# Gate operands and the stored product on GpSimd's queue, and the last gate tile in two column halves: a hybrid encoder block on one core

## The chip, the cores and the metric

The kernel runs on one core of a Trainium2 chip. The core has a matrix engine (TensorE, PE in the profile, with PEld for its weight loads), a vector engine (VectorE, DVE), a scalar engine (ScalarE, ACT), GpSimd (POOL) and SyncE (SP), each with its own queue of instructions that it works off in order. SP computes nothing here; it issues DMAs. POOL can issue DMAs too. Whoever issues them, 16 DMA engines move the data. The metric is the device time of one execution in microseconds; lower is better.

## What is computed

The reference is one encoder block over 1024 tokens of width 1024: windowed attention and a recurrent mixer side by side, an output projection, a feed-forward part, and at the end a gated input embedding. The change touches the two last parts, which are:

```python
        x = x + merged @ w_out[i]
        hf = rms_norm(x, norm_ffn[i])
        x = x + jnp.square(jax.nn.relu(hf @ w_ff1[i])) @ w_ff2[i]
        hp = rms_norm(x, norm_ple[i])
        x = x + (p[i] @ w_ple[i]) * jax.nn.sigmoid(hp @ w_ple_gate[i])
```

Here `w_ff2` is 4096 x 1024, `w_ple_gate` is 1024 x 1024, `p` is 1024 x 256 and `w_ple` is 256 x 1024.

## The kernel before

**Products.** All data are float32. Each matrix operand is split into a high part (ACT casts it, L205) and a low part (DVE subtracts, L206), and a product is three matmuls: high by high, high by low, low by high. The three large products at the end are done as block products with seven multiplications instead of eight (quarter blocks B11 to B22 and sums of them, named T1 to T4 and S1 to S4).

**Second feed-forward product** (from about 1210 us to 1530 us). Seven products (`PRODS`, numbered `ip` 0 to 6) run one after the other, each over 16 steps p. A step fetches a left tile of hidden values from DRAM (`sst`, three slots, L1834 in `fetch`), splits it into `sh` and `sl`, makes the right tile from a fetched weight block (`tst`, three slots) or from sums that are kept on the chip, splits it into `th` and `tl`, and runs 12 matmuls (L2024) on it. The split tiles have five slots each (`NR2`). After a product, DVE adds its four banks to the residual `X` (L1881).

**Gate operands.** The seven right operands of the gate product depend on weights alone. They are made while products 1 to 4 run: the generator `gate_operands` is advanced by one piece after some of the steps. A piece loads a raw block of 128 x 512 (`graw`, three slots, L1896), or forms a sum on DVE (`gsum`, two slots), and `keep` splits it with the same `th` and `tl` slots and stores the two parts in DRAM (`gop_d`, L1900). In all there are 16 loads and 56 stores of 256 KB. During product 6 and later they are loaded again (L1962, on SP's queue).

**Stored product.** During product 6, `ple_product` computes `p @ w_ple` for eight groups of tokens, and ACT scales it by 0.5 (L2006). The 16 results go to DRAM (`pw_d`, L2007).

**Gate product and end** (from about 1555 us). `product_of` runs 12 matmuls into one bank, for each of four groups of 128 tokens and each product. `finish` does the rest for a tile of 128 tokens by 512 columns, 16 times: it loads the stored product (`pwl`, three slots, L2112), applies tanh on ACT (L2113), multiplies on DVE (L2114), adds to `X` on DVE (L2115), and stores the output (L2116). `add_bank` (L2105) adds the last bank to the kept partial sum before that. The sigmoid is written as (tanh(x/2) + 1)/2, and the factor one half is in the stored product.

**Order.** The program is traced in the order of the code; a planner then lays out each engine's queue from dependencies, slots and its own costs, so instructions of different steps are mixed, and it also picks the slot of each tile. Matmuls marked by `keep_in_program_order` (`mmo`) stay in the order of the code. A queue is worked off in order: a DMA that waits for its data or for a free slot holds all DMAs behind it on that queue. Before the change, SP's queue holds the fetches of the feed-forward product, the gate loads and stores, the stored product in both directions, and the output. POOL's queue holds at this stage only the small `rstd` steps of the last norm (L189). Earlier in the kernel POOL issues some DMAs as well (L226, L413, L415, L777, L929).

Of the kernel before, what the change touches and what calls it, by code (L numbers as in the profile page):

```python
# [9 lines left out]
F32 = mybir.dt.float32  # L10
F32R = mybir.dt.float32r
AF = mybir.ActivationFunctionType
ALU = mybir.AluOpType
# [4 lines left out]
P = 128  # L18
# [131 lines left out]
def block_kernel(ctx: ExitStack, tc: tile.TileContext, I: dict, out: bass.AP):  # L150
    nc = tc.nc

    def pool(stack, name, bufs=1, **kw):
        return stack.enter_context(tc.tile_pool(name=name, bufs=bufs, reuse_waits="tile", **kw))
# [20 lines left out]
    gop_d = {r: DR.tile([2, P, 4, 512], F32, name="gop_" + r) for r in ("T1", "T4", "B11", "T2", "T3", "B22", "B21")}  # L175
    pw_d = DR.tile([NT, 2, P, 512], F32, name="pw_d")
# [69 lines left out]
    def mm3(ps, pairs):  # L246

        n = len(pairs)
        for i, (ah, al, bh, bl) in enumerate(pairs):
            nc.tensor.matmul(ps, ah, bh, start=(i == 0), stop=False)  # L250
            nc.tensor.matmul(ps, ah, bl, start=False, stop=False)  # L251
            nc.tensor.matmul(ps, al, bh, start=False, stop=(i == n - 1))  # L252
# [95 lines left out]
    with ExitStack() as s0:  # L348
# [51 lines left out]
        parts = []  # L400
# [50 lines left out]
        for t in range(NT):  # L451
# [34 lines left out]
            r = QW.tile([P, NQK], F32, name="r2", bufs=2)  # L486
# [433 lines left out]
    with ExitStack() as s2:  # L920
# [16 lines left out]
        for n in range(NT):  # L937
# [5 lines left out]
            for kv in range(2):  # L943
# [6 lines left out]
                for h in range(4):  # L950
                    sc = PA.tile([P, nk * P], F32, name="sc", tag="sc", bufs=2)
                    for j in range(2):
                        nc.tensor.matmul(sc, qT[:, 4 * kv + h, :], kT[:, kv, j, k0 * P:k1 * P], start=(j == 0), stop=(j == 1))
                    nc.vector.tensor_tensor_reduce(
                        out=sm[:, h, 0:nk * P], in0=sc, in1=band[:, b0:b0 + nk, :].rearrange("p b t -> p (b t)"), scale=1.0,
                        scalar=-3.0e38, op0=ALU.add, op1=ALU.max, accum_out=mx[:, h:h + 1])
# [629 lines left out]
    with ExitStack() as s7:  # L1586
# [15 lines left out]
        for j, i in enumerate((4, 5, 6, 7, 0, 1, 2, 3)):  # L1602
            t = torder[i]
# [10 lines left out]
        raw = [NR.tile([P, 4, 512], F32, name=f"raw{k}", bufs=1) for k in range(2)]  # L1614
# [50 lines left out]
        for i in range(NT):  # L1665
# [6 lines left out]
            t = torder[i]  # L1672
# [23 lines left out]
    def tmp(name, bufs=1):  # L1696
        return FP.tile([P, 512], F32, name=name, bufs=bufs)
# [58 lines left out]
    for p in range(NPR):  # L1756
# [13 lines left out]
        else:  # L1770
            s_ = tmp("u2")
# [55 lines left out]
    def parts_of(pl, names, src_, bufs):  # L1827
        hi, lo = (pl.tile([P, 512], F32R, name=x_, bufs=bufs) for x_ in names)
        split(hi, lo, src_)
        return hi, lo  # L1830
# [20 lines left out]
    def acc(bs, name="ff2ps"):  # L1851
        return PH.tile([P, 512], F32, name=name, tag=f"acc{bs}", bufs=4)

    def sum_of(op, a_, b_, out_=None):
        o_ = F2.tile([P, 512], F32, name="tmp", bufs=2) if out_ is None else out_
        nc.vector.tensor_tensor(out=o_, in0=a_, in1=b_, op=op)
        return o_
# [28 lines left out]
    def gate_block(k, b):  # L1886
        r = (k + 4 * (int(b[1]) - 1)) * P
        n = 512 * (int(b[2]) - 1)
        return I["w_ple_gate"][r:r + P, n:n + 512]

    def gate_operands():

        def load(k, b):
            if k < 4:
                raw[b] = QP.tile([P, 512], F32, name="graw", tag="graw", bufs=3)
                nc.sync.dma_start(raw[b], gate_block(k, b))  # L1896

        def keep(k, r, src_):
            for x_, t_ in enumerate(parts_of(F2, ("th", "tl"), src_, NR2)):
                nc.sync.dma_start(gop_d[r][x_][:, k, :], t_.bitcast(F32))  # L1900

        def gsum():
            return QP.tile([P, 512], F32, name="gsum", tag="gsum", bufs=2)

        raw = {}
        for b in ("B11", "B12", "B22"):
            load(0, b)
        yield
        for k in range(4):
            t = sum_of(ALU.subtract, raw["B12"], raw["B11"], gsum())  # L1910
            keep(k, "T1", t)
            yield
            keep(k, "B11", raw["B11"])
            load(k, "B21")
            yield
            keep(k, "T3", sum_of(ALU.subtract, raw["B22"], raw["B12"], gsum()))
            load(k + 1, "B11")
            yield
            sum_of(ALU.subtract, raw["B22"], t, t)
            keep(k, "T2", t)  # L1920
            yield
            keep(k, "B22", raw["B22"])
            load(k + 1, "B12")
            yield
            sum_of(ALU.subtract, raw["B21"], t, t)
            keep(k, "T4", t)
            yield
            keep(k, "B21", raw["B21"])
            load(k + 1, "B22")
            yield  # L1930

    def tok(e, i):
        t = torder[4 * e + i]
        return X[e][:, i, :], slice(t * P, (t + 1) * P), t
# [64 lines left out]
    def ple_product(k, pp):  # L1999

        for n in range(2):
            pw = acc(1, "pwps")
            nsl = slice(512 * n, 512 * n + 512)
            mm3(pw, [(pp[0][:, j, :], pp[1][:, j, :], wp[0][:, j, nsl], wp[1][:, j, nsl]) for j in range(2)])
            t_ = F2.tile([P, 512], F32, name="pwt", tag="tmp", bufs=2)
            nc.scalar.activation(out=t_, in_=pw, func=AF.Copy, scale=0.5)  # L2006
            nc.sync.dma_start(pw_d[k, n], t_)  # L2007

    gops = gate_operands()
    GL, GR = {}, {}  # L2010
# [1 line left out]
    for ip, (lr_, rr_, bs, fresh) in enumerate(PRODS):  # L2012
        if fresh:
            banks[bs] = [acc(bs) for _ in range(4)]
        for p in range(NPR):
# [25 lines left out]
            if ip == 1 and p % 2 == 0:  # L2041
                e, i = divmod(p // 2, 4)
                t = torder[4 * e + i]
# [8 lines left out]
            if ip == 5 and p % 4 == 1:  # L2052
                k, nsl = p // 8, slice(512 * (p // 4 % 2), 512 * (p // 4 % 2) + 512)
                split(wp[0][:, k, nsl], wp[1][:, k, nsl], fetch(F2, wpv[:, k, nsl], "tst", 3))
            if ip == 6:
                next(gl[p // 8], None)
                if p % 2 == 0 and p < 8:
                    ple_norm(1, p // 2)
                if p % 2 == 1 and 2 < p < 11:
                    second_tokens((p - 3) // 2)  # L2060
                if p >= 7:
                    pps.append(ple_p(p - 7)) if p < 15 else None
                    if p > 7:
                        ple_product(p - 8, pps[p - 8])
        for i in range(4):
            b_ = banks[bs][i]
# [26 lines left out]
    LP = pool(sF, "gate2")  # L2093
    GL["A11"], GR["B11"] = left(LP, 2), gate_loaded(LP, 2, "B11")
    g12 = LP.tile([P, 4, 512], F32, name="g12", bufs=1)
    cs_ = {n: [LP.tile([P, 512], F32, name=n, tag=f"{n}{i}", bufs=1) for i in range(4)] for n in ("gc5", "gc4", "gc1", "gu2")}

    def product_of(bank, l, r, i, fresh=True):
        (lh, ll), (rh, rl) = GL[l], GR[r]
        for k in range(4):  # L2100
            for j, (x_, y_) in enumerate(((lh, rh), (lh, rl), (ll, rh))):
                mmo(bank, x_[:, k, tsl(i)], y_[:, k, :], start=fresh and k + j == 0, stop=k == 3 and j == 2, skip_group_check=True)

    def add_bank(n, i, bank):
        nc.vector.tensor_tensor(out=cs_[n][i], in0=cs_[n][i], in1=bank, op=ALU.add)  # L2105

    def finish(e, n, i, c):

        xv, rows, t = tok(e, i)
        nsl = slice(512 * n, 512 * n + 512)  # L2110
        pw = LP.tile([P, 512], F32, name="pwl", bufs=3)
        nc.sync.dma_start(pw, pw_d[t, n])  # L2112
        nc.scalar.activation(out=c, in_=c, func=AF.Tanh, scale=0.5)  # L2113
        nc.vector.scalar_tensor_tensor(out=c, in0=c, scalar=1.0, in1=pw, op0=ALU.add, op1=ALU.mult)  # L2114
        nc.vector.tensor_tensor(out=xv[:, nsl], in0=xv[:, nsl], in1=c, op=ALU.add)  # L2115
        nc.sync.dma_start(out[rows, nsl], xv[:, nsl])  # L2116

    R4 = range(4)
    ple_norm(0, 0)
# [1 line left out]
    kept = [acc(1, "gps5") for _ in R4]  # L2121
# [8 lines left out]
    for i in R4:  # L2130
        b_ = acc(0, "gps4")
# [6 lines left out]
    chain = [acc(0, "gps1") for _ in R4]  # L2138
# [15 lines left out]
    for i in R4:  # L2154
        product_of(chain[i], "S3", "T3", i, False)
        for e, n, c in ((1, 1, "gc5"), (1, 0, "gc4")):
            add_bank(c, i, chain[i])
            finish(e, n, i, cs_[c][i])
    for i in R4:
        product_of(kept[i], "S4", "B22", i, False)  # L2160
        add_bank("gu2", i, kept[i])
        finish(0, 1, i, cs_["gu2"][i])
    for i in R4:
        b_ = acc(0, "gps2")
        product_of(b_, "A12", "B21", i)
        add_bank("gc1", i, b_)
        finish(0, 0, i, cs_["gc1"][i])
    sF.close()
    sRP.close()
    sX.close()  # L2170
# [25 lines left out]
```

## Time and profile before

| | us |
|---|---|
| median of three runs | 1649.55 |
| lowest and highest run | 1646.11, 1649.56 |
| the profiled execution | 1649.13 |
| its span, first to last instruction | 1647.4 |
| PE busy in the span | 1595.4 |
| mean granted clock of TensorE | 0.991 of full speed |

The profile is of one execution. Its span is shorter than its time by what lies around it. PE's share of the span, 97%, is an average: most stretches have no gap at all, and a few have all of them. Windows of 20 us show which. A row of the table of windows gives the busy time and the number of instructions of each engine, and then the granted clock, the share of the DMA engines and the bytes moved in GB/s. A row of the timeline gives start, duration, engine, line, operation and tiles; brackets hold the idle time of that engine before it and what ended it. A row of waits gives who waited for whom: total, times and the longest.

### The profile page before, as it was taken

The numbers are of one execution on the slowest core, as the hardware profiler recorded it, in microseconds if no ns is written. First come the engines' busy times: TensorE is split into PE (matmuls) and PEld (weight loads), VectorE is DVE, ScalarE is ACT, GpSimd is POOL, SyncE is SP. The second block draws the span as 40 slices with busy tenths as digits, with TensorE's granted clock in tenths as the row PEclk, the third lists the DMA queues.
The fourth block names the chain that finished last, engine by engine and source line by source line (L and its number), as shares of the span: only waits on it lengthen the run. The fifth ranks groups of instructions, "written<-read, shape, count | busy, mean of one in ns | idle before, by whom it ended". The sixth has DMA issues, their size and how long they took to land.

```text
span 1647.4 us, 31465 instructions
## 1 busy us (share of the span) xinstructions
PE 1595.4 (97%) x12232; PEld 1289.4 (78%) x12232; DVE 1176.3 (71%) x2161; ACT 874.5 (53%) x1615; POOL 84.6 (5%) x110
## 2 busy tenths in 40 slices
PE   7999999999999999899999999999999999999998
PEld 7987777767768777667888788888888778788886
DVE  6758998378849769688737876676758868777257
ACT  5558888388554563655314544444444444546352
POOL 1430000300000000000001000000000000000000
PEclk9999999999989999999999999999999999999999
DMA  6363555964575744567822354444479887768356
GB/s 228 84 159 109 167 166 180 274 165 141 157 198 172 217 147 130 165 194 247 271 79 92 119 169 156 159 145 145 151 261 315 278 275 239 238 218 286 125 198 236
DMA packets 218678, 307.02 MB, mean 186 GB/s; under 512 B 49824, under 2 KB 106016, under 8 KB 217248
## 3 DMA queue, kind: packets, MB, share of 16 engines
q1 hardware_dynamic: 207312, 287.70, 53.8%
q0 software_dynamic: 11072, 16.78, 3.8%
q8 instruction: 96, 1.57, 0.4%
q10 hardware_dynamic: 144, 0.52, 0.1%
q14 instruction: 54, 0.44, 0.1%
HBM read 205.33 MB, written 99.61 MB: 185 GB/s over the span
## 4 chain that ended last, share of the span: by engine, by line
PE 66%; DVE 16%; DMA 8%; ACT 6%; issue 3%; POOL 1%; SPq 0%; DVEq 0%; ACTq 0%; POOLq 0%
PE ff1ps L1694 16%; PE ff2ps L2024 12%; PE gps L232 4%; PE uaps L232 2%; DMA wst<-in_w_col_dram 2%; DVE Z L1346 2%; DVE tmp L1343 2%; PE mm L250 2%; DMA tst<-in_w_ff_dram 2%; PE mm L251 2%; PE mm L252 2%; PE gmm L232 2%; PE mmo L251 1%; PE mmo L252 1%; PE mmo L250 1%
## 5 line engine op out<-in xcount | busy, mean ns | idle before, releaser
L2024 PE MATMUL ff2ps<-th,sh 128*128 128x512 f32 x448 | 177.2, 396 | 5.7 <-ACT th L205 5.7
L2024 PE MATMUL ff2ps<-tl,sh 128*128 128x512 f32 x448 | 178.0, 397 | 4.1 <-DVE tl L206 4.0
L2024 PE MATMUL ff2ps<-th,sl 128*128 128x512 f32 x448 | 176.6, 394 | 0.0
L2024 PEld LDWEIGHTS ff2ps<-th,sh 128*128 128x128 f32 x448 | 85.4, 191 | 25.7 <-ACT th L205 7.7
L2024 PEld LDWEIGHTS ff2ps<-tl,sh 128*128 128x128 f32 x448 | 85.4, 191 | 24.8 <-DVE tl L206 6.9
L205 ACT CAST whi<-wst 128x512 fp32r<-128x512 f32 x100 | 60.0, 618 | 83.6 <-DMA wst<-in_w_col_dram 34.1
L205 ACT CAST sh<-sst 128x512 fp32r<-128x512 f32 x109 | 67.2, 619 | 62.8 <-DMA sst<-hid_A 22.2
L2024 PEld LDWEIGHTS ff2ps<-th,sl 128*128 128x128 f32 x448 | 85.7, 191 | 17.7
L206 DVE TENSOR_TENSOR sl<-sst,sh 128x512 fp32r<-128x512 f32 x109 | 74.7, 687 | 24.0 <-ACT sh L205 23.6
L1694 PE MATMUL ff1ps<-mh,w1h 128*128 128x512 f32 x224 | 87.5, 391 | 0.2 <-ACT w1h L205 0.2
L1694 PE MATMUL ff1ps<-ml,w1h 128*128 128x512 f32 x224 | 87.4, 390 | 0.0
L1694 PE MATMUL ff1ps<-mh,w1l 128*128 128x512 f32 x224 | 87.2, 389 | 0.0
L205 ACT CAST w1h<-w1st 128x512 fp32r<-128x512 f32 x48 | 28.4, 620 | 99.8 <-DMA w1st<-in_w_ff_dram 62.0
L206 DVE TENSOR_TENSOR wlo<-wst,whi 128x512 fp32r<-128x512 f32 x88 | 58.9, 685 | 16.9 <-ACT whi L205 14.8
L206 DVE TENSOR_TENSOR w1l<-w1st,w1h 128x512 fp32r<-128x512 f32 x48 | 31.9, 687 | 51.3 <-ACT w1h L205 51.3
L189 POOL TENSOR_TENSOR rstd<-ms,neghalf 128x1 f32<-128x1 f32 x24 | 15.4, 643 | 1000.5 <-issue 589.3
L1208 DVE TENSOR_TENSOR gm<-gps,gmask 128x384 f32<-128x384 f32 x64 | 32.8, 551 | 31.0 <-PE gps L232 30.9
L232 PE MATMUL gmm<-hh,wlo 128*128 128x512 f32 x128 | 53.4, 417 | 0.0
L238 PE MATMUL gmm<-hh,whi 128*128 128x512 f32 x128 | 51.5, 402 | 1.7 <-ACT whi L205 1.7
L232 PE MATMUL gmm<-hl,whi 128*128 128x512 f32 x128 | 53.2, 415 | 0.0
L206 DVE TENSOR_TENSOR w1l<-ssum,w1h 128x512 fp32r<-128x512 f32 x64 | 42.9, 687 | 14.3 <-ACT w1h L205 14.3
L232 PE MATMUL gmm<-hh,whi 128*128 128x512 f32 x128 | 53.0, 414 | 0.0
(463 smaller groups left out, 4593.8 us busy)
## 6 DMA issues: line engine op xcount, KB each, us to landing
tst<-in_w_ff_dram SPq DMA_DIRECT2D x80, 256.0 KB, 4.5
wst<-in_w_col_dram SPq DMA_DIRECT2D x76, 256.0 KB, 3.8
w1st<-in_w_ff_dram SPq DMA_DIRECT2D x32, 512.0 KB, 4.9
hid_S<-h SPq DMA_DIRECT2D x64, 256.0 KB, 2.1
sst<-hid_S SPq DMA_DIRECT2D x64, 256.0 KB, 4.2
hid_A<-h SPq DMA_DIRECT2D x48, 256.0 KB, 2.0
sst<-hid_A SPq DMA_DIRECT2D x45, 256.0 KB, 4.2
ra_d<-ra SPq DMA_DIRECT2D x8, 1024.0 KB, 5.9
```

The lines of the kernel that those rows point to most:

```text
L205: a = nc.scalar.copy(hi, src)
L206: b = (lo_eng or nc.vector).tensor_tensor(out=lo, in0=src, in1=hi.bitcast(F32), op=ALU.subtract)
L232: tc.keep_in_program_order(nc.tensor.matmul(*a, **kw))
L238: mm(ps, ah, bh, start=(i == 0), stop=False)
L250: nc.tensor.matmul(ps, ah, bh, start=(i == 0), stop=False)
L251: nc.tensor.matmul(ps, ah, bl, start=False, stop=False)
L252: nc.tensor.matmul(ps, al, bh, start=False, stop=(i == n - 1))
L1208: a = (nc.vector.tensor_tensor(out=gm[hf][:, s % NB, e].rearrange("p (a b) t -> p a b t", b=2), in0=pss[e][:, 0:6].rearrange("p (a b) t -> ...
L1343: turn(nc.vector.tensor_tensor(out=tv, in0=Lp[:, t + 1:32, t:t + 1].broadcast_to([P, n, m]), in1=Z[:, t:t + 1, 0:m].broadcast_to([P, n, m] ...
L1346: turn(nc.vector.tensor_tensor(out=Z[:, t + 1:32, 0:m], in0=Z[:, t + 1:32, 0:m], in1=tv, op=ALU.add))
L1694: (mmo if p < 2 else nc.tensor.matmul)(ps, x_[:, k, :], y_[:, k, :], start=start and k + i == 0, stop=k == 3 and i == 2, skip_group_check= ...
L2024: nc.tensor.matmul(banks[bs][i], x_[:, isl], y_, start=fresh and p + j == 0, stop=p == NPR - 1 and j == 2, skip_group_check=True)
```

## The change

The loads of raw gate blocks, the stores of gate operands, and the stores and loads of the stored product are issued by GpSimd (POOL) instead of SP. `add_bank` is folded into `finish`, which issues the load of the stored product ahead of the add; `pwl` has four slots instead of three. The very last tile is finished in two halves of 256 columns, each with its own add, tanh, multiplication, sum and output store.

```diff
         def load(k, b):
             if k < 4:
                 raw[b] = QP.tile([P, 512], F32, name="graw", tag="graw", bufs=3)
-                nc.sync.dma_start(raw[b], gate_block(k, b))
+                nc.gpsimd.dma_start(raw[b], gate_block(k, b))
 
         def keep(k, r, src_):
             for x_, t_ in enumerate(parts_of(F2, ("th", "tl"), src_, NR2)):
-                nc.sync.dma_start(gop_d[r][x_][:, k, :], t_.bitcast(F32))
+                nc.gpsimd.dma_start(gop_d[r][x_][:, k, :], t_.bitcast(F32))
...
-            nc.sync.dma_start(pw_d[k, n], t_)
+            nc.gpsimd.dma_start(pw_d[k, n], t_)
...
-    def add_bank(n, i, bank):
-        nc.vector.tensor_tensor(out=cs_[n][i], in0=cs_[n][i], in1=bank, op=ALU.add)
-
-    def finish(e, n, i, c):
+    def finish(e, n, i, name, bank, parts=1):
 
         xv, rows, t = tok(e, i)
-        nsl = slice(512 * n, 512 * n + 512)
-        pw = LP.tile([P, 512], F32, name="pwl", bufs=3)
-        nc.sync.dma_start(pw, pw_d[t, n])
-        nc.scalar.activation(out=c, in_=c, func=AF.Tanh, scale=0.5)
-        nc.vector.scalar_tensor_tensor(out=c, in0=c, scalar=1.0, in1=pw, op0=ALU.add, op1=ALU.mult)
-        nc.vector.tensor_tensor(out=xv[:, nsl], in0=xv[:, nsl], in1=c, op=ALU.add)
-        nc.sync.dma_start(out[rows, nsl], xv[:, nsl])
+        c = cs_[name][i]
+        pw = LP.tile([P, 512], F32, name="pwl", bufs=4)
+        nc.gpsimd.dma_start(pw, pw_d[t, n])
+        w = 512 // parts
+        for o in range(0, 512, w):
+            s_, xs = slice(o, o + w), slice(512 * n + o, 512 * n + o + w)
+            nc.vector.tensor_tensor(out=c[:, s_], in0=c[:, s_], in1=bank[:, s_], op=ALU.add)
+            nc.scalar.activation(out=c[:, s_], in_=c[:, s_], func=AF.Tanh, scale=0.5)
+            nc.vector.scalar_tensor_tensor(out=c[:, s_], in0=c[:, s_], scalar=1.0, in1=pw[:, s_], op0=ALU.add, op1=ALU.mult)
+            nc.vector.tensor_tensor(out=xv[:, xs], in0=xv[:, xs], in1=c[:, s_], op=ALU.add)
+            nc.sync.dma_start(out[rows, xs], xv[:, xs])
...
         for e, n, c in ((1, 1, "gc5"), (1, 0, "gc4")):
-            add_bank(c, i, chain[i])
-            finish(e, n, i, cs_[c][i])
+            finish(e, n, i, c, chain[i])
     for i in R4:
         product_of(kept[i], "S4", "B22", i, False)
-        add_bank("gu2", i, kept[i])
-        finish(0, 1, i, cs_["gu2"][i])
+        finish(0, 1, i, "gu2", kept[i])
     for i in R4:
         b_ = acc(0, "gps2")
         product_of(b_, "A12", "B21", i)
-        add_bank("gc1", i, b_)
-        finish(0, 0, i, cs_["gc1"][i])
+        finish(0, 0, i, "gc1", b_, 2 if i == 3 else 1)
```

## The prediction

> **What bounds the kernel now.** I begin with the first lines of the page: the span, and the busy time of each engine.
>
> ```profile
> span 1647.4 us, 31465 instructions
> ...
> PE 1595.4 (97%) x12232; PEld 1289.4 (78%) x12232; DVE 1176.3 (71%) x2161; ACT 874.5 (53%) x1615; POOL 84.6 (5%) x110
> ```
>
> TensorE (PE) sets the time almost everywhere, and the change takes no matmul away. So it can only shorten stretches in which PE waits. The change touches the kernel from about 1288 us on. The table of windows shows where PE is not full there (columns: window, length, busy us and instructions of PE, PEld, DVE, ACT, POOL, granted clock, DMA share, GB/s). The first row is a loaded stretch ahead of the gate work, for comparison; the last row is taken up further down.
>
> ```profile
> 1210.00:1280.00 70.00, 70.00 (x310) 57.86 (x310) 54.41 (x87) 32.80 (x55) 0.00 (x0) 1.00 0.94 325
> ...
> 1300.00:1320.00 20.00, 16.83 (x62) 12.19 (x61) 15.62 (x25) 9.09 (x16) 0.00 (x0) 0.91 0.83 277
> ...
> 1340.00:1360.00 20.00, 16.62 (x64) 13.00 (x65) 14.29 (x24) 9.74 (x17) 0.00 (x0) 0.91 0.85 261
> ...
> 1400.00:1420.00 20.00, 16.86 (x62) 13.10 (x61) 14.14 (x23) 9.42 (x17) 0.00 (x0) 0.83 0.80 254
> ...
> 1297.00:1346.00 49.00, 42.68 (x172) 32.60 (x170) 31.70 (x51) 21.36 (x38) 0.00 (x0) 0.97 0.84 275
> ```
>
> I call the three stalls A (1300 to 1320), B (1340 to 1360) and C (1400 to 1420). PE is idle for 3.17, 3.38 and 3.14 us in them. Behind each one the granted clock is low for a while: 0.09, 0.09 and 0.17 of 20 us, so 1.8, 1.8 and 3.4 us more. A and B together cost 10.2 us and C 6.5 us. These 16.7 us are the most that the moved DMAs can give back here.
>
> Next the waits of SP's own queue, in the window 1280 to 1440 (total, times, longest):
>
> ```profile
> SPq L1900 <- ACT th L205: 30.4, 22, 3.2
> ...
> SPq L1900 <- DVE tl L206: 12.6, 26, 1.7
> SPq L1896 <- DVE gsum L1856: 6.3, 4, 2.2
> ```
>
> For 49.3 of 160 us the queue stands still at a gate store or a gate load, whose data or slot is not ready. Every fetch behind it (L1834: `sst`, `tst`) waits too, although it needs neither. The timeline shows this ahead of each stall (start, duration, engine, instruction, and in brackets the idle time before it and what ended that).
>
> ```profile
> 1298.43 0.44 SPq L1834 DMA_DIRECT2D tst<-in_w_ff_dram  x1
> ...
> 1299.15 0.68 DVE L206 TENSOR_TENSOR tl<-tst,th 128x512 fp32r<-128x512 f32 x1
> ...
> 1301.53 0.32 SPq L1900 DMA_DIRECT2D gop_B<-th  x1
> ...
> 1306.21 0.45 SPq L1834 DMA_DIRECT2D tst<-in_w_ff_dram  x1
> ...
> 1311.82 0.62 ACT L205 CAST th<-tst 128x512 fp32r<-128x512 f32 x1 [1.89 <-DMA tst<-in_w_ff_dram]
> ...
> 1312.49 0.50 PE L2024 MATMUL ff2ps<-th,sh 128*128 128x512 f32 x1 [1.70 <-ACT th L205]
> ```
>
> Stall A: `tst` has three slots. The read at 1299.15 frees one at 1299.83, and the fetch that lands there leaves only at 1306.21, 6.4 us later. ACT and then PE wait for its landing.
>
> ```profile
> 1332.01 0.68 DVE L206 TENSOR_TENSOR sl<-sst,sh 128x512 fp32r<-128x512 f32 x1
> ...
> 1336.42 0.33 SPq L1896 DMA_DIRECT2D graw<-in_w_ple_gate_dram  x1
> ...
> 1337.68 0.33 SPq L1900 DMA_DIRECT2D gop_B<-th  x1
> ...
> 1338.86 0.45 SPq L1834 DMA_DIRECT2D sst<-hid_A  x1
> ...
> 1342.75 0.62 ACT L205 CAST sh<-sst 128x512 fp32r<-128x512 f32 x1 [3.70 <-DMA sst<-hid_A]
> ...
> 1345.77 0.49 PE L2024 MATMUL ff2ps<-th,sh 128*128 128x512 f32 x1 [3.15 <-ACT th L205]
> ```
>
> Stall B: the `sst` slots of the reads up to 1332.01 are free by 1332.69, and the fetch leaves at 1338.86, behind a gate load and two gate stores. ACT sits idle for 3.70 us, and PE follows.
>
> ```profile
> 1387.76 2.29 SPq L1834 DMA_DIRECT2D tst<-in_w_ff_dram  x1
> ...
> 1388.57 0.61 ACT L205 CAST th<-gsum 128x512 fp32r<-128x512 f32 x1
> ...
> 1392.04 0.39 SPq L1900 DMA_DIRECT2D gop_T<-th  x1
> ...
> 1397.17 0.32 SPq L1900 DMA_DIRECT2D gop_B<-th  x1
> ...
> 1401.88 0.62 ACT L205 CAST th<-gsum 128x512 fp32r<-128x512 f32 x1 [3.69 <-DMA gop_B<-th]
> ...
> 1406.27 0.80 PE L2024 MATMUL ff2ps<-tl,sh 128*128 128x512 f32 x1 [2.70 <-DVE tl L206]
> ```
>
> Stall C is the other way round. The `th` tile is ready at 1389.18, but its store leaves 2.86 us later, because SP stood at fetches, the first of which held it from 1387.76 to 1390.05. The gate work slips, and ACT then waits for a `th` slot until the next store has landed.
>
> **The change, part by part.** *Queue moves.* 16 gate loads, 56 gate stores, 16 stores and 16 loads of the product go from SP to POOL's queue. No bytes are added. SP keeps `sst`, `tst` and the output, so its fetches wait for their own slots alone; on POOL only gate transfers and 6 small `rstd` (L189) stand behind a waiting store. The stores of the product and four of its loads may stand ahead of the last two `rstd`, but those are needed only for the transposes of later tiles; I price this at nothing, and at 1 to 2 us if that cover is gone. What does a transfer on POOL's queue cost? Three rows are nearest: the same weight load on either queue, and POOL's issue of a store (KB and median us to landing; then ns min/median/max).
>
> ```profile
> wst<-in_w_col_dram SPq DMA_DIRECT2D x76, 256.0 KB, 3.8
> ...
> wst<-in_w_col_dram POOLq DMA_DIRECT2D x16, 256.0 KB, 4.6
> ...
> L413 POOL DMA_DIRECT2D qT_d<-qkT x16: 533/579/728, 36.5 to 110.0; - x16
> ```
>
> So 0.8 us more to landing, and 0.58 us of POOL, which is idle here: 104 issues take 60 us of some 350. A POOL landing could be no later at all (it then no longer queues behind SP's transfers) or, where it meets full DMA engines, later than 0.8; I take 0.8, the like-for-like pair.
>
> A and B: the late fetches leave 4 to 6 us earlier, more than the 1.7 to 3.2 us for which PE waited. Then the DMA engines are next. The window 1297 to 1346 moves 275 GB/s x 49 us = 13.5 MB. Without its 10.2 us of stalls it would need 347 GB/s, and the loaded stretch at 1210 kept up 325, which makes 41.5 us instead of 38.8: 2.7 us come back. POOL's queue also uses more engine time for a byte; its rows in the window 262 to 330 (packets, MB, share):
>
> ```profile
> q1 hardware_dynamic: 13640, 11.41, 55.3%
> q0 software_dynamic: 2880, 4.72, 24.7%
> ```
>
> That is 4.85% for a MB on SP's and 5.23% on POOL's, 8% more. About half of the 13.5 MB moves over: 0.08 x half of (0.84 x 49) = 1.6 us. A and B keep 4.3 of 10.2 us; the gain is 6 us (bounds 0 and 10.2).
>
> C: the store leaves 2.9 us earlier, against PE waits of about 3.1 us; two stores in the chain land 0.8 us later. Some 2 us remain, with or without a low clock behind them (A shows it behind a wait of 1.70). I take a gain of 4 us (bounds 0 and 6.5).
>
> *The last stretch.* Output stores and product loads leave each other's queue, and there are four slots instead of three. These rows carry the price:
>
> ```profile
> 1625.85 0.69 DVE L2114 SCALAR_TENSOR_TENSOR gc<-gc,pwl 128x512 f32<-128x512 f32 x1 [1.20 <-DMA pwl<-pw_d]
> ...
> 1639.22 0.39 PE L232 MATMUL gps<-grh,glgs 128*128 128x512 f32 x1
> ...
> 1641.50 0.68 DVE L2105 TENSOR_TENSOR gc<-gc,gps 128x512 f32<-128x512 f32 x1
> ...
> 1643.60 0.69 DVE L2115 TENSOR_TENSOR X<-X,gc 128x512 f32<-128x512 f32 x1
> ...
> L205 ACT CAST pp<-pt x8: 395/396/408, 1393.8 to 1549.2; 128x256 fp32r<-128x256 f32 x8
> L206 DVE TENSOR_TENSOR pp<-pt,pp x8: 418/426/427, 1394.5 to 1549.7; 128x256 fp32r<-128x256 f32 x8
> ```
>
> The last matmul ends at 1639.6, and DVE adds its bank 1.9 us later, as it is behind; at least 1.2 us of that is waiting for a product load. I take 1.4 us (0 to 1.9). From that add to the end of the last one are 2.8 us. In halves a DVE step takes about 0.42 and an ACT step 0.40 us; with the halves interleaved, six DVE steps and one wait for ACT make about 2.5 us (0.3 gained); one half after the other makes 2 x 1.7 = 3.4 (0.6 lost). The final store has half the bytes and I count nothing for it. Together 1.7 us (-0.6 to 2.2).
>
> Sum: 6 + 4 + 1.7 = 11.7 us. The profiled execution took 1649.13 us (its span and 1.7 us around it), 0.4 below the median 1649.55. So 1637.4 against the former, and 1638 us against the latter. The bounds: everything gained is 18.9, so 1630.6; nothing and the tail worse, 1650.
>
> **The rivals.** *The DMA engines become the bound.* For: the shares above. If the share cannot pass 0.94, the window needs (0.84 x 49 + 1.6)/0.94 = 45.5 us: 3.5 gained, C keeps its wait for a store, the tail gives 1.7: 1644 (1642 to 1646). Against: before each stall SP was waiting, not the engines.
>
> *Only issue time is saved.* The waits move to POOL, SP then waits for slots that come free no earlier, and the fetches leave when they did. Only the tail counts: 1648 (1646 to 1651). Against: the 6 us between free slot and fetch. The Trainium skill (DMA: Bandwidth & Descriptors, section "Issuing engines are not separate DMA queues") holds that all issuers share the same 16 engines and that spreading saves only sequencer time; by that rule this rival is right. The trace does not bear it out: what SP loses is 49 us of waiting in order.
>
> *Slower: POOL's stores land late and hold the `th` and `tl` slots.* ACT already waits for them:
>
> ```profile
> ACT th L205 <- DMA gop_B<-th: 12.4, 9, 3.7
> ```
>
> Five slots serve the gate tiles and PE's operands alike. If a store takes some 1.5 us longer rather than 0.8, ACT's lead is used up at the gate tiles; A and B return as waits for slots, and one more stall like C costs 6.5 us: 1649.5 + 6.5 - 1.7 = 1654 (1651 to 1660). For: 28 such pairs, DMA share 0.8. Against: POOL's 0.58 us issues. The Trainium skill (SBUF — State Buffer, section "Who interferes with whom") says that descriptors of POOL's DMAs can starve while DVE runs in a two-port mode, but that `tensor_tensor` has none; no run here shows starving, and if it came it would be this rival.
>
> **How the numbers follow.** Forecast 0.50 (1630 to 1642), DMA bound 0.18, issue time only 0.16, slower 0.16. The range 1630 to 1653 leaves out the upper part of the last. A measurement of this kernel can tell about 0.2% (3.3 us) from no change, so faster is below 1646.3 and slower above 1652.8: 0.68 faster, 0.17 same, 0.15 slower.
>
> **What would show it.** Right: SP's waits at L1900 and L1896 gone, to POOL; windows of 20 us from 1300 to 1420 with 19 us or more of PE and clock 1.00; `sst` and `tst` issued within 1 us of a free slot; the last add within 0.5 us of the last matmul. Wrong: ACT's waits for `gop` stores above 30 us in sum; DMA share over 0.95 with ACT still waiting for `sst`; POOL landings of 5 us and more. Since the planner lays out a new order for all engines when queues change, a stall at a new place would also make it wrong.

## The result: slower, and where the time went

| | before | after |
|---|---|---|
| median of six runs, us | 1648.69 | 1661.96 |
| lowest and highest, us | 1646.11, 1651.07 | 1658.27, 1667.22 |
| span of the profiled execution, us | 1647.4 | 1659.7 |
| after to before, with its 95% interval | | 1.0081 (1.0062 to 1.0101) |

The change costs 13 us. The first lines of the page of the changed kernel:

```profile
span 1659.7 us, 31568 instructions
...
PE 1599.7 (96%) x12232; PEld 1291.6 (78%) x12232; DVE 1175.5 (71%) x2164; ACT 872.8 (53%) x1616; POOL 141.3 (9%) x214
```

The same matmuls run, so again only PE's waits matter. Of the 12.3 us of span, 11.6 lie in the second feed-forward product (the starts of its first and last matmul are 346.6 us apart before and 358.2 after; before, its last matmul starts at 1556.4 us, later than the 1530 named above). It starts 2.5 us later; the kernels below start it anywhere from 1208.5 (loads_t4own2) to 1213.3 (gate_pool), both with gate loads on POOL, so this is put down to the spread between executions, though that is not shown. The end got 1.9 us shorter. The windows of the changed kernel, in which the reader should look at the number of matmuls behind PE's busy time (90 is full):

```profile
1300.00:1320.00 20.00, 17.58 (x71) 14.10 (x70) 12.96 (x22) 7.23 (x14) 3.78 (x7) 0.91 0.73 238
1320.00:1340.00 20.00, 17.47 (x74) 13.25 (x73) 9.98 (x16) 7.02 (x13) 4.32 (x8) 1.00 0.84 261
1340.00:1360.00 20.00, 16.54 (x68) 12.27 (x67) 10.77 (x18) 9.25 (x17) 4.33 (x8) 1.00 0.71 251
...
1400.00:1420.00 20.00, 14.01 (x54) 9.93 (x54) 13.94 (x25) 8.95 (x17) 4.71 (x9) 0.95 0.76 256
...
1280.00:1460.00 180.00, 161.50 (x665) 127.84 (x664) 123.09 (x199) 78.24 (x141) 36.76 (x68) 0.96 0.71 232
```

and the last of these windows in the kernel before:

```profile
1280.00:1460.00 180.00, 170.18 (x710) 136.55 (x709) 139.10 (x224) 85.52 (x151) 0.00 (x0) 0.96 0.77 252
```

None of the three stalls went away, and 1320 to 1340, full before, lost matmuls too. A matmul takes 70 us / 310 = 0.226 us in the loaded stretch of before that the prediction quotes. 710 - 665 = 45 matmuls fewer are 10.2 us: here is the loss. The DMA engines are less busy than before (0.71 for 0.77). Next, who waited for whom between 1280 and 1460 (total, times, longest), first before the change:

```profile
ACT sh L205 <- DMA sst<-hid_A: 14.4, 7, 3.7
ACT th L205 <- DMA gop_B<-th: 13.7, 10, 3.7
ACT sh L205 <- DMA sst<-hid_S: 12.6, 9, 3.6
ACT th L205 <- DMA tst<-in_w_ff_dram: 10.8, 7, 3.3
...
ACT th L205 <- DMA gop_T<-th: 5.9, 8, 1.4
...
DVE tl L206 <- DMA gop_B<-tl: 5.3, 4, 1.7
DVE tl L206 <- DMA gop_T<-tl: 4.5, 5, 2.3
```

and after it:

```profile
ACT th L205 <- DMA gop_T<-th: 25.4, 9, 4.4
ACT th L205 <- DMA gop_B<-th: 22.9, 7, 4.7
...
ACT sh L205 <- DMA sst<-hid_S: 4.9, 6, 1.4
...
DVE tl L206 <- DMA gop_T<-tl: 18.2, 9, 3.6
DVE tl L206 <- DMA gop_B<-tl: 14.7, 8, 4.5
...
PE ff2ps L2024 <- DVE tl L206: 16.7, 14, 3.4
...
SPq L1834 <- DVE sl L206: 100.1, 49, 6.1
```

The fetches did become early. ACT's waits for them fell from 14.4 + 12.6 + 10.8 = 37.8 us to 8.0 in all, and SP now waits for free slots at its fetches. But ACT's and DVE's waits for gate stores rose from 19.6 and 9.8 us to 48.3 and 32.9. A wait of a cast for a store is a wait for a slot: the tile about to be written still has to be read out by the store of an earlier gate piece. One instance from the timeline of the changed kernel:

```profile
1333.68 0.62 ACT L205 CAST th<-graw 128x512 fp32r<-128x512 f32 x1
...
1334.60 0.54 POOL L1900 DMA_DIRECT2D gop_B<-th  x1 [6.62 <-ACT th L205]
...
1334.73 0.62 ACT L205 CAST th<-tst 128x512 fp32r<-128x512 f32 x1
...
1340.09 0.62 ACT L205 CAST th<-gsum 128x512 fp32r<-128x512 f32 x1 [4.74 <-DMA gop_B<-th]
...
1341.04 0.69 DVE L206 TENSOR_TENSOR tl<-gsum,th 128x512 fp32r<-128x512 f32 x1 [4.48 <-DMA gop_B<-tl]
1341.14 0.61 ACT L205 CAST th<-tst 128x512 fp32r<-128x512 f32 x1
...
1341.80 0.50 PE L2024 MATMUL ff2ps<-th,sh 128*128 128x512 f32 x1 [0.58 <-ACT th L205]
...
1343.17 0.68 DVE L206 TENSOR_TENSOR tl<-tst,th 128x512 fp32r<-128x512 f32 x1
...
1343.91 0.50 PE L2024 MATMUL ff2ps<-tl,sh 128*128 128x512 f32 x1 [1.61 <-DVE tl L206]
```

The gate piece cast at 1333.68 is stored from 1334.60 on. The cast of the next piece needs its slot and stands at the head of ACT's queue until 1340.09; DVE stands in the same way at that piece's `tl`. Behind both stand the operands of PE (`th<-tst` at 1341.14, `tl<-tst` at 1343.17), which need no gate data. PE waits for these.

The end of the kernel went as forecast:

```profile
1653.37 0.39 PE L232 MATMUL gps<-grh,glgs 128*128 128x512 f32 x1
...
1654.33 0.75 DVE L2113 TENSOR_TENSOR gc<-gc,gps 128x256 f32<-128x256 f32 x2
...
1655.96 0.75 DVE L2116 TENSOR_TENSOR X<-X,gc 128x256 f32<-128x256 f32 x2
```

The last matmul ends at 1653.76 and DVE adds its bank 0.57 us later, not 1.9. The span ends 5.9 us behind the last matmul, and did so 7.8 us behind it before.

### The profile page after: what moved, and what is told of

It is laid out like the page before. It is cut to its first block, busy times and chain, and to the rows that moved or that the text cites. A ratio compares the mean times of both kernels' runs of the same rounds, so it can differ in the third digit from the quotient of the medians.

```text
span 1659.7 us, 31568 instructions
## 1 busy us (share of the span) xinstructions
PE 1599.7 (96%) x12232; PEld 1291.6 (78%) x12232; DVE 1175.5 (71%) x2164; ACT 872.8 (53%) x1616; POOL 141.3 (9%) x214
## 4 chain that ended last, share of the span: by engine, by line
PE 66%; DVE 10%; DMA 9%; issue 7%; ACT 6%; POOL 2%; DVEq 0%; SPq 0%; POOLq 0%; ACTq 0%
PE ff1ps L1694 16%; PE ff2ps L2024 8%; PE gps L232 5%; PE gmm L232 4%; DMA wst<-in_w_col_dram 2%; PE mm L250 2%; PE mm L251 2%; PE mm L252 2%; PE psq L468 1%; PE psq L470 1%; PE psq L469 1%; PE mmo L252 1%; PE mmo L250 1%; PE mmo L251 1%; PE wy L232 1%
## 5 line engine op out<-in xcount | busy, mean ns | idle before, releaser
L232 PE MATMUL gmm<-hh,wlo 128*128 128x512 f32 x128 | 53.2, 416 | 0.0
L242 PE MATMUL gmm<-hh,wlo 128*128 128x512 f32 x128 | 51.6, 403 | 0.7 <-POOL wlo L206 0.5
```

Of the source, the lines that this page charges most:

```text
L232: tc.keep_in_program_order(nc.tensor.matmul(*a, **kw))
L242: mm(ps, al, bh, start=False, stop=(i == n - 1))
```

## The experiments

Three theories stood against each other. **Slots:** POOL's stores hold the shared `th` and `tl` slots longer, and the gate pieces and all behind them wait. **Order:** a change of queue makes the planner lay out new orders for ACT and DVE, and these cost. **DMA engines:** POOL's transfers load them more. All runs, with the ratio to the kernel before on the same chip; the last three columns are sums of the rows of waits between 1280 and 1460 (gop: rows of `th`, `gth` and of `tl`, `gtl` for gate stores; fetch: ACT's rows for `sst` and the `tst` of `w_ff2`), beside PE's matmuls there:

| kernel | us | ratio (95%) | matmuls | ACT gop | DVE gop | fetch |
|---|---|---|---|---|---|---|
| before | | 1 | 710 | 19.6 | 9.8 | 37.8 |
| after | 1661.96 | 1.0081 (1.0062 to 1.0101) | 665 | 48.3 | 32.9 | 8.0 |
| gate_pool | 1656.33 | 1.0065 (1.0041 to 1.0088) | 669 | 49.1 | 33.5 | 10.0 |
| tail_only | 1644.05 | 0.9984 (0.9969 to 0.9998) | 722 | 17.7 | 5.6 | 38.5 |
| loads_pool | 1651.34 | 1.0032 (1.0016 to 1.0047) | 701 | 46.9 | 7.2 | 15.3 |
| stores_pool | 1661.34 | 1.0074 (1.0045 to 1.0104) | 650 | 45.7 | 36.6 | 17.3 |
| after_t4own2 | 1665.76 | 1.0111 (1.0090 to 1.0133) | 715 | 5.3 | 10.3 | 18.2 |
| after_even | 1661.33 | 1.0082 (1.0056 to 1.0107) | 660 | 61.3 | 31.6 | 10.4 |
| tail_t4own2 | 1640.80 | 0.9959 (0.9943 to 0.9975) | 759 | 11.1 | 3.9 | 18.8 |
| after_t6s4 | 1669.01 | 1.0126 (1.0102 to 1.0150) | 655 | 56.9 | 29.2 | 6.8 |
| stores_t4own2 | 1661.06 | 1.0091 (1.0064 to 1.0117) | 674 | 6.7 | 18.8 | 4.1 |
| loads_t4own2 | 1650.58 | 1.0030 (1.0015 to 1.0045) | 705 | 31.1 | 6.1 | 11.3 |
| after_small | 1642.33 | 0.9974 (0.9960 to 0.9989) | 738 | 32.8 | 12.9 | 8.7 |
| after_thonly | 1652.41 | 1.0035 (1.0016 to 1.0053) | 703 | 47.4 | 0 | 9.8 |
| pool_order_before | 1655.02 | 1.0051 (1.0034 to 1.0069) | 678 | 54.1 | 24.4 | 9.6 |
| after_order_before | 1653.68 | 1.0039 (1.0024 to 1.0053) | 687 | 55.2 | 30.9 | 10.2 |
| sp_order_pool | 1659.10 | 1.0066 (1.0043 to 1.0089) | 734 | 39.5 | 9.7 | 22.2 |
| own_pool_order | 1641.25 | 0.9966 (0.9952 to 0.9980) | 748 | 5.6 | 8.6 | 14.9 |
| small_order_before | 1634.94 | 0.9935 (0.9912 to 0.9958) | 784 | 30.3 | 9.4 | 12.1 |
| after_own_order | 1642.17 | 0.9973 (0.9958 to 0.9987) | 733 | 9.7 | 8.2 | 24.9 |

**The parts of the change, one at a time.** gate_pool is the kernel before with both gate lines moved, loads_pool and stores_pool with one of them; tail_only is the changed kernel with both back on SP, so only the stored product's transfers, the fourth `pwl` slot and the halves are left.

```diff
-                nc.sync.dma_start(raw[b], gate_block(k, b))
+                nc.gpsimd.dma_start(raw[b], gate_block(k, b))
-                nc.sync.dma_start(gop_d[r][x_][:, k, :], t_.bitcast(F32))
+                nc.gpsimd.dma_start(gop_d[r][x_][:, k, :], t_.bitcast(F32))
```

> Only the gate operands' loads and stores move to POOL's queue; the product's transfers and the last stretch stay as before. Slots (the gate stores on POOL's queue hold th and tl slots until they have landed): about 1664 us, that is the changed kernel's 1662 without the 1.9 us that its last stretch gained; ACT's waits for gate stores near 48 us in the stage. If the loss sat in the product's transfers on POOL's queue instead: about 1649 us.

> Only the product's transfers move to POOL's queue, with the fourth slot and the two halves; the gate operands stay on SP's queue. Slots: about 1647 us, 1.5 to 2 below before, and 5.9 us from the last matmul to the end in place of 7.8. If the product's transfers cause the loss: about 1660 us.

> Only the 16 gate loads move to POOL's queue. Slots: 1645 to 1650 us, since loads hold no th or tl slot. DMA engines (POOL's transfers cost more engine time for a byte): 16 of 72 gate transfers, so 16/72 of the 13 us, about 1652 us. Planner (any queue move lays out a new order, and the new order is what costs): anything, a loss of 5 to 15 us as likely here as with the stores.

> Only the 56 gate stores move to POOL's queue. Slots: the whole loss, 1660 to 1666 us, with ACT's waits for gate stores at 40 us or more. DMA engines: 56 of 72 transfers, about 1659 us, with ACT waiting for sst and tst. Planner: not tied to the stores.

The end is worth 0.16% and the gate transfers cost. gate_pool has the waits that were expected (49.1 us) but is 8 us faster than expected. The stores alone cost as much as both; the loads cost about half. In loads_pool the stores are on SP as before, and still ACT's waits for them rose to 46.9 us; DVE's did not (7.2). In these kernels, where ACT alone waits at a slot, less is lost than where DVE waits too.

**Slots of their own, more slots, pieces further apart.** after_t4own2 gives the gate pieces two slots of their own (own2 below) and PE's operands four; tail_t4own2 is the same with the gate transfers on SP. after_t6s4 has six shared slots for `th`, `tl` and four for `sh`, `sl`. after_even spreads the 28 pieces evenly over the 48 steps of products 2 to 4.

```diff
-    NPRE, NR2, T1EARLY = 3, 5, 8
+    NPRE, NR2, T1EARLY = 3, 4, 8
-            for x_, t_ in enumerate(parts_of(F2, ("th", "tl"), src_, NR2)):
+            for x_, t_ in enumerate(parts_of(QP, ("gth", "gtl"), src_, 2)):
```

> The changed kernel, with two slots of their own for the gate pieces (gth, gtl) and four instead of five for PE's th, tl, sh, sl. Slots theory: a gate cast now waits for the store of two pieces back, 5.4 us of steps against a turn of 4.5 us, so ACT's waits for gop stores fall from 48 us to under 15 and DVE's from 33 to under 10 (window 1280 to 1460), and the time from 1662 to 1645-1651. Planner's order alone: the waits stay somewhere in the order, 1656-1668. DMA engines: same bytes on the same queues, 1657 or more.

> The changed kernel with its 28 gate pieces spread evenly over the 48 steps of the three products, instead of runs of three steps in five; five shared slots as before. Slots theory: pieces come at least one free step apart as a rule (4.66 us on average against a turn of 4.5), ACT's waits for gop stores fall from 48 us to under 25, and the time to 1648-1655. Planner's order alone: no direction, 1650-1668. DMA engines: the load is spread more evenly but the bytes of the stretch stay, 1656 or more.

> Gate transfers on SP as before the change, the product's on POOL, with the own two slots for the gate pieces. Slots theory: ACT's waits for gop stores fall (17.7 us in the kernel without own slots) to under 6, but SP still stands at gate transfers, so fetches are late as before: 1640-1645. Planner's order: 1642-1660. DMA engines: 1644.

> The changed kernel with six th, tl slots instead of five (and four sh, sl instead of five, to make room). Slots theory, as 'fewer slots than needed': if the planner keeps putting a gate piece into the slot of the piece before, the waits stay (over 35 us of ACT, 1655-1663); if it rotates, they fall under 25 us and the time to 1647-1655. DMA engines: 1657 or more either way.

Three misses for the slots theory as it stood. In after_t4own2 the waits for gate stores were down to 5.3 and 10.3 us, and yet the kernel was slower than the changed one. Its gate pieces began at 1215 us instead of 1297, and in 1220 to 1280 it ran 180 matmuls where tail_t4own2 ran 265: with free slots and loads on POOL the planner had moved gate work 80 us forward. after_even had even more waits (the planner does not keep to the spacing of the code), and after_t6s4 only exchanged one wait for another (PE waited 12.9 us for `sl`, which had lost a slot). On SP the own slots gave 0.9959, with 11.1 us of ACT's gop waits left where under 6 was expected: the fastest kernel of those that store whole gate pieces.

**Which part, with own slots; fewer bytes; fewer stores.** stores_t4own2 and loads_t4own2 move one line each of tail_t4own2 to POOL. after_small stores 128 of the 512 columns; after_thonly leaves out the stores of the low parts.

> Own two slots for the gate pieces and four for the operands; gate loads on SP, gate stores and the product's transfers on POOL. Slots theory: with slots of their own the later landing of POOL's stores touches only the gate pieces, which start where SP's loads let them (about 1298 us): 1635-1645, as fast as the same kernel with its stores on SP (1640.8). Theory that stores on POOL cost by themselves, whatever the slots: 1650 or more. Placement theory (the order laid out for POOL's loads starts gate work 80 us early, on full DMA engines): fast here too, since the loads are on SP.

> The counterpart: own slots, gate loads on POOL, gate stores on SP. Placement theory: first gate cast near 1215 us instead of 1298, DMA share 0.98 and more from 1220 to 1300, PE waits there, 1650-1666. Slots theory alone: 1635-1645.

> The changed kernel with only the first 128 of 512 columns of each gate piece stored (the gate operands are then read back from those columns, so the gate products are other numbers): a quarter of the bytes, the same number of issues, loads and waits. Slots theory: landings fall from 3.2-4.4 us to about 2.5, a turn from 4.5 to about 3, ACT's and DVE's waits for gop stores from 81 us in sum to under 40, time 1640-1650. Planner's order alone: 1655-1665. DMA engines: share under 0.7 everywhere and time 1640-1650, but with fetch waits falling rather than the gop waits.

> The changed kernel without the 28 stores of the gate pieces' tl parts (the operands' low parts are read from the stored th, so the gate products are other numbers). Slots theory: DVE's waits for gop<-tl (33 us) are gone, PE's waits for DVE tl (16.7 us) fall under 6, ACT's waits for th stores stay or fall a little; time 1643-1652. Planner's order alone: 1655-1665.

stores_t4own2 went against the slots theory: with own slots, moving nothing but the gate stores cost 20 us. after_small and after_thonly went with it in their times (after_thonly just above its range) but not in all their waits: after_small kept 45.7 us of waits for gate stores where under 40 was expected, and in after_thonly PE still waited 12.4 us for `tl` where under 6 was expected. loads_t4own2 was 0.7% slower than tail_t4own2, but only its first two pieces were early (the third cast stands at 1299.63), so the placement theory does not explain it. In all of these the order of ACT and DVE differed from kernel to kernel, so queue and order were mixed.

**Order and queue parted.** The next kernels pin the sequence of instructions of ACT, DVE and PE, and of what stays on SP, to that of another kernel. `ORDER` is that kernel's sequence, as numbers. The slots of the tiles are not pinned; the planner still picks them.

```python
    made = {i.name: i for i in nc.cur_bb.bb.instructions}
    for row in ORDER:
        row = [x for x in row if f"I-{x}" in made]
        for a, b in zip(row, row[1:]):
            tc.add_manual_dep(made[f"I-{b}"], f"I-{a}", mybir.DependencyInfo(mybir.DependencyClass.NoSync, mybir.DependencyReason.DATA), reason="order")
```

> Gate loads and stores on POOL's queue, and ACT, DVE, PE and the rest of SP in exactly the order of the kernel before. Order theory (the new order costs, not the queue): SP's waits at gate transfers are gone and nothing takes their place, 1634-1646. Queue theory (POOL's stores react and land later): ACT's and DVE's waits for gop stores grow as in the changed kernel (over 60 us in sum), 1650-1662.

> The other way round: gate transfers on SP as before the change, with ACT, DVE and PE in exactly the order of gate_pool (gate loads and stores on POOL, 1656). Order theory: as slow as gate_pool or slower, 1652-1665. Queue theory: 1642-1652.

> stores_t4own2 (1661) with ACT, DVE, PE and SP in the order of tail_t4own2 (1641): two slots of their own for the gate pieces, their stores on POOL. Order theory: 1630-1642. Queue theory: 1652-1663.

> The whole change, with ACT, DVE, PE and the rest of SP in the order of the kernel before up to the last gate tiles. Order theory: 1632-1644 (pool_order_before less the 1.9 us of the last stretch). Queue theory: 1650-1664.

pool_order_before is the kernel before with the gate transfers on POOL and the other queues in their old order. It is 8.6 us slower. The waits of ACT and DVE in it and the row of the window:

```profile
ACT th L205 <- DMA gop_T<-th: 29.2, 11, 5.1
ACT th L205 <- DMA gop_B<-th: 24.9, 9, 4.2
...
DVE tl L206 <- DMA gop_T<-tl: 15.0, 9, 3.7
DVE tl L206 <- DMA gop_B<-tl: 9.4, 5, 3.9
...
1280.00:1460.00 180.00, 163.80 (x678) 126.41 (x678) 126.34 (x205) 78.58 (x142) 37.29 (x69) 0.99 0.70 232
```

So with shared slots the move costs even in the old order: fetch waits fell by 28 us, gop waits of ACT and DVE grew by 34 and 15, and 32 matmuls (7.2 us) fewer fit.

But the queue is not the only thing that differs. In the kernels as the planner laid them out, the `th` slot of a gate piece is written again by the second `th` cast after it for 17 of the 28 pieces before and for 26 in pool_order_before (by the third for the others), and the `tl` slot by the second `tl` after it for 6 and for 13. A slot that is written again sooner makes the cast wait longer for the same store. Two kernels have such slots for `th` and their gate stores on SP as before: loads_pool (25 of 28) and sp_order_pool (26 of 28). ACT waits 46.9 and 39.5 us for gate stores in them, against 19.6 before. So a large part of ACT's waits goes with the slots. DVE's waits go with the queue, as far as the table shows: 3.9 to 9.8 us in all kernels with the gate stores on SP, 24.4 us and more in those with all stores whole, on POOL and in shared slots. How the 8.6 us divide between queue and slots stays open.

Two of the landing rows, before and in pool_order_before (KB, median us from issue to landing):

```profile
gop_T<-th SPq DMA_DIRECT2D x16, 256.0 KB, 3.3
gop_T<-tl SPq DMA_DIRECT2D x16, 256.0 KB, 3.5
```

```profile
gop_T<-th POOLq DMA_DIRECT2D x16, 256.0 KB, 3.8
gop_T<-tl POOLq DMA_DIRECT2D x16, 256.0 KB, 4.2
```

They are 0.5 and 0.7 us later (the stores to `gop_B` 0.3 later and 0.1 earlier). To this comes a later start. From the end of a cast to the start of its store pass 0.03 us on SP (median of 28) and 0.29 us on POOL, and the issue itself takes 0.54 us for 0.32.

With own slots the picture turns. stores_t4own2 and own_pool_order have the same queues and the same number of slots and differ in order (the split tiles lie in the same slots in both; of the fetched tiles some `tst` and `graw` do not). Their waits of DVE, first of stores_t4own2, then of own_pool_order:

```profile
DVE gtl L206 <- DMA gop_T<-gtl: 12.6, 8, 3.8
DVE gtl L206 <- DMA gop_B<-gtl: 6.2, 4, 2.4
```

```profile
DVE gtl L206 <- DMA gop_T<-gtl: 6.7, 4, 3.3
...
DVE gtl L206 <- DMA gop_B<-gtl: 1.9, 3, 1.3
```

In the order of tail_t4own2 the stores on POOL cost nothing that can be measured (0.9966 against 0.9959 on SP, the intervals overlap); here every split and fetched tile has the same slot in both kernels, so only the queue differs. So the 20 us of stores_t4own2 went with its order. The whole change in the order of before (after_order_before) is 1.0039, in its own order 1.0081, and the intervals are apart: its order, with the slots picked in it, costs 0.42%, 6.9 us (by the two intervals some 4 us more or less), beside the move.

sp_order_pool missed both expectations for a reason of its own. With the order of gate_pool a gate load stood on SP ahead of the fetches, far from the gate stores:

```profile
1225.04 8.42 SPq L1896 DMA_DIRECT2D graw<-in_w_ple_gate_dram  x4
```

```profile
1232.56 0.79 PE L2024 MATMUL ff2ps<-tl,sh 128*128 128x512 f32 x1 [11.51 <-DVE tl L206]
```

The window 1220 to 1240 had 31 matmuls of 90, 59 x 0.226 = 13.3 us, more than the whole difference. Between 1280 and 1460 it had 734, more than before. So gate_pool's order is not shown to cost in the gate stretch, and on POOL that order and the order of before gave the same within their intervals (1.0065, 1.0051).

**Smaller stores in the old order.** small_order_before is pool_order_before with a quarter of each store; a second edit, not shown, makes the loads that bring the operands back (L1962) read that quarter four times. after_own_order is after_t4own2 in the order of tail_t4own2.

```diff
-                nc.gpsimd.dma_start(gop_d[r][x_][:, k, :], t_.bitcast(F32))
+                nc.gpsimd.dma_start(gop_d[r][x_][:, k, 0:128], t_[:, 0:128].bitcast(F32))
```

> pool_order_before with only the first 128 of 512 columns of each gate piece stored and read back (the gate products are other numbers); order, queue, issues and slots the same. Shared slots held by late landings: landings fall from 3.4-4.2 us to about 2.5, ACT's and DVE's waits for gop stores from 78 us to under 45, time from 1655 to 1638-1646. Something else on POOL's queue (its reaction, its issues, its standing in order): 1650-1656.

> after_t4own2 (1666) with ACT, DVE, PE and the rest of SP in the order of tail_t4own2: the whole change, with two slots of their own for the gate pieces. Order theory: 1636-1645. If the loads on POOL cost by themselves: 1650 or more.

With order, queue and number of DMAs unchanged, the kernel fell from 1655 to 1635, a little below what was expected. Rows of small_order_before:

```profile
gop_T<-th POOLq DMA_DIRECT2D x16, 64.0 KB, 3.2
gop_T<-tl POOLq DMA_DIRECT2D x16, 64.0 KB, 2.4
...
1280.00:1460.00 180.00, 179.00 (x784) 146.61 (x784) 149.16 (x242) 92.38 (x168) 37.21 (x69) 1.00 0.65 204
```

PE is nearly full. The gop waits fell from 54.1 and 24.4 to 30.3 and 9.4 us, while the fetch waits (9.6 and 12.1) did not fall. So it is the slots that came free sooner; they are written again no later than in pool_order_before (by the second cast for 27 of 28 `th` and 17 of 28 `tl`). The run also takes bytes off the DMA engines (0.70 to 0.65), so how much of the shorter landing is size and how much a lighter load it does not tell. after_own_order, at 0.9973, has the whole change with own slots and the order of tail_t4own2: the loads on POOL are not shown to cost either (own_pool_order, with the loads on SP, is 0.9966). But no kernel with whole stores shows a gain from the move: tail_t4own2, with its gate transfers on SP, is as fast.

## Why the prediction was wrong, step by step

- **SP's waits in order** (49.3 us at gate transfers, fetches 4 to 6 us late): right. They are gone, and ACT's fetch waits went from 37.8 to 8.0 us.
- **A and B, a gain of 6 us:** here it failed, at the sentence "Then the DMA engines are next." The next thing late was the slot of the gate piece: ACT's and DVE's waits for gate stores rose from 19.6 and 9.8 to 48.3 and 32.9 us. The stalls stayed (71 and 68 matmuls in the two windows, 62 and 64 before), a third one came between, and the DMA share fell. The size of the stalls was about right: by the count of matmuls A, B and C are 28, 26 and 28 short of 90, which is 18.5 us where 16.7 were priced. small_order_before shows that the slots stood in the way: with a quarter of each store the same move, in the same order, gives 0.65%. With whole stores the gain was not had in any kernel; in the changed one 45 matmuls, 10.2 us, were lost where the sum had 10 us gained at A, B and C.
- **C, a gain of 4 us:** failed in the same way. What an earlier store could give was lost again at the slots; 54 matmuls for 62.
- **The price of a transfer on POOL, 0.8 us:** about right in size. In the same order the landing is 0.5 and 0.7 us later for the `gop_T` stores, and the start 0.26. But it was read as a loss of 0.8 us at one place, C. It lengthens the turn of every gate piece whose slot is waited for. From the end of a gate cast to the start of the next one, where that one waited for a gate store, the median is 3.66 us before (7 casts) and 4.53 after (10), with 4.08 in pool_order_before (11), and everything behind in ACT's and DVE's queues comes later by it.
- **The slower rival** had the right mechanism: waits for `th` and `tl` slots. It put the turning point at about 1.5 us later and its time at 1654. The landings came 0.5 and 0.7 us later, and the order of before on POOL gave 1655.0 and 1653.7. That time is in part luck: the rival counted on late landings alone, and the slots of gate pieces were also picked to be written again sooner (26 of 28 `th` by the second cast, 17 before). The prediction had the row of 12.4 us of ACT waiting for `gop_B` in hand: these slots were tight already. A chance of 0.16 was too little.
- **The new order** was named last, as what would make the prediction wrong, and had no price. With the slots picked in it, it cost 6.9 us of the 13. That the planner also picks other slots when queues change has no place in the prediction.
- **The end, 1.7 us:** right, 1.9 measured.
- **The DMA engines as the bound:** not so. SP waits for slots, not engines, and their share fell.
- **Only issue time is saved:** not so. In pool_order_before, in an unchanged order, ACT's waits for fetches fell by 28 us, and SP's waits at L1900 and L1896 are gone. The Trainium skill (DMA: Bandwidth & Descriptors, section "Issuing engines are not separate DMA queues") has it that spreading over issuers saves only sequencer time; the measurement says more was saved here, and then lost at the slots.

What stays open: which feature of the new orders costs; whether later start, longer issue or later landing on POOL weighs most; and how much of the loss in the old order is the queue and how much the slots that are written again sooner. A kernel with its slots pinned as well as its order would tell; none was run.

## What to carry to other kernels

Before a wait is taken out of one queue, list the waits right behind it by resource, slots included, and ask for each how much lead is left: a store that holds a slot shared with the operands of the bounding engine is on its path. Moving a DMA to another queue also reorders other engines wherever a planner lays them out; pin the order and the slots in one experiment, or the costs of queue, order and slots can't be told apart. Here the cure is a slot ring of its own for what is stored (0.9959 with the gate transfers on SP, and no cost of the queue left).

## What was not expected of the hardware

- GpSimd starts a waiting store about 0.29 us after the instruction that it waits for has ended, SyncE 0.03 us, and issues it in 0.54 us instead of 0.32.
- PE's busy time hides short gaps. pool_order_before is idle for 180 - 163.8 = 16.2 us, but 678 matmuls are 797 - 678 = 119 short of full (180 / 0.226 = 797), 26.9 us. The mean clock of this window is 0.99, so the clock does not explain it. Count the matmuls.
- Many short waits left the granted clock alone. pool_order_before has 24 waits of PE of at most 1.7 us and a clock of 0.99; the kernel before has 9 waits of up to 3.2 us and 0.96.
